# Whose engine subtracts the low halves: u, v and latent input projection weights, GpSimd to VectorE

## The chip, the cores and the metric

The kernel runs on one core of one Trainium2 chip. The core has a matrix engine (TensorE, "PE" in the profile, its weight loads "PEld"), VectorE ("DVE"), ScalarE ("ACT"), GpSimd ("POOL") and a queue that issues transfers (SyncE, "SP"). The metric is the time of one execution on the device in microseconds, the median of the runs.

## The reference

One layer of a hybrid diffusion backbone is applied to 256 context tokens and 1024 latent tokens with a model width of 1024. A token passes through a modulated norm, one input projection, windowed attention and a recurrent branch, an output projection with residual, a second norm, and a retrieval over 16384 experts. Each of 8 heads picks 16 experts e with weights g, and the mixer adds

```python
u = jnp.take(u_tab, eid, axis=0)
act = jax.nn.gelu(jnp.einsum('td,thkd->thk', xb, u))
vv = jnp.take(v_tab, eid, axis=0)
return jnp.einsum('thk,thkd->td', g * act, vv)
```

All of it is in float32.

## The kernel before

**Products in three passes.** TensorE carries a 12-bit mantissa exactly in one pass, so `split` (L132) writes an operand as a sum of two parts: ScalarE copies it into the high half (L134), and another engine subtracts the high half from the operand (L135). `mm3` (L138 to L140) then makes three products: high by high, high weights by low, low weights by high. The engine of the subtract is the fourth argument of `split`: VectorE if none is given. Before the change, GpSimd subtracts for five kinds of operand: the weights of the latent input projection (`wl`, 14 tiles), the weights of the retrieval's queries (`wl` too, 32 tiles), the experts' rows `ul` (128 tiles) and `vl` (128 tiles). VectorE does so for the other operands, among them `al`, the gated activations, and the context projection's weights (`wl`, 14 tiles). All weight tiles have 128 partitions by 1024 columns.

**Two ways to compute the experts.** For six of the eight latent tiles of 128 tokens (768 tokens) all 16384 experts are computed densely on TensorE, in 128 chunks of 128 experts: `experts_in` makes u products (16 groups of 3 matmuls of 384 columns for a chunk, 48 in all), gelu on ScalarE (L756), the weights g (L757, VectorE), a split of the result, and 36 matmuls of 512 columns against v (tiles `res`, which stay in PSUM, and `rot`, which are copied out by ScalarE at L737 and added to `acc` by VectorE at L738). The other four tiles (two of context, two of latent tokens) gather the 128 chosen rows of u and of v for each token: GpSimd issues an indirect DMA for each (L826, L837), and VectorE does a multiply with sum (L829) or a multiply-add (L843) on the row, 128x1024 elements each. Up to seven rows are in flight.

**Order.** The stages run in this order: modulations, the context's own layer up to its picks, the latent input projection with the recurrent branch, attention, output projection and norm, the retrieval's queries, the spreading of the weights (`spread`), with the u products of the first 34 chunks taken ahead (from about 980 to 1670 us), and `dense` (from about 1695 us): 17 pairs of chunks whose u products are already there, then 47 pairs that still make theirs. The program is written in one order, and a planner puts each engine's instructions in a fixed order from its own estimate of durations; each engine then works in that order and waits for the others by semaphores. The gathers are paced by hand: `tick` counts microseconds of other work and lets the generator `mix` issue the next row when enough have gone by; the row's VectorE work is queued behind a VectorE instruction of the dense part (`paced`).

Two loaded tiles of u and of v are there at a time, two of `uh` and `ul`, three of `vh` and `vl`, and one of `w` in the latent projection.

Of the kernel before, what the change touches and what calls it, by code (L numbers as in the profile page):

```python
# [18 lines left out]
PSUM = bass.MemoryType.PSUM  # L19
# [3 lines left out]
D = 1024  # L23
# [13 lines left out]
SCALE = HD ** -0.5  # L37
# Pairs (a, b) of ranks that can be among the 16 largest sums: (a + 1)(b + 1) <= 16.
SEGS = [(0, 1, 16), (1, 1, 8), (2, 1, 5), (3, 1, 4), (4, 1, 3), (5, 3, 2), (8, 8, 1)]
NC = sum(n * b for _, n, b in SEGS)  # L40
# Latent tiles whose experts are computed densely on the tensor engine; the others gather rows.
N_DENSE = 6
N_GATHER = N_LAT - N_DENSE
TD = N_DENSE * P
# Dense output tiles that stay in PSUM, chunks of experts whose products share an accumulation, chunks
# whose first products are taken ahead, gathered rows in flight (and more of them beside the dense part).
N_RES = 2
# [3 lines left out]
N_MORE = 3  # L51
# Pacing of the gathers: microseconds of other work per row and per part of that work.
F_STEP = 1.9
# [4 lines left out]
PE_US = 15.8  # L58
# The engine that divides a head's row by its sum.
NORM = "AAGV"  # L60
# [4 lines left out]
def body(ctx: ExitStack, tc: tile.TileContext, i, o):  # L65
# [44 lines left out]
    def tick(us, ins=None):  # L110
        """Gathers that may run beside us microseconds of the other work."""
        clock[0] += us
        if ins is not None:
            behind.append(ins.ins)
        ph = cur[0]
        step = D_STEP if ph == "dense" else STEP.get(ph, F_STEP)
        while queue and clock[0] >= step:
            try:
                next(queue[0])
                clock[0] -= step  # L120
            except StopIteration:
                queue.pop(0)
        if not queue:
            clock[0] = 0.0
# [7 lines left out]
    def split(hi, lo, src, eng=None):  # L132
        """src as the sum of two parts of 12 bits that one pass of a product carries exactly."""
        A.activation(hi, src, AF.Copy)  # L134
        return (eng or V).tensor_tensor(lo, src, hi, op=OP.subtract)  # L135
# [6 lines left out]
    def rstd_of(ss, p):  # L142
        """(ss / D + EPS) ** -0.5, with a Newton step."""
        m = p.tile([P, 1], F32, name="rs_m", bufs=3)
        V.tensor_scalar(m, ss, 1.0 / D, EPS, op0=OP.mult, op1=OP.add)
        r = p.tile([P, 1], F32, name="rs_r", bufs=3)
        G.tensor_tensor(r, m, nhalf, op=OP.pow)
        s = p.tile([P, 1], F32, name="rs_s", bufs=3)
        V.tensor_scalar(s, r, r, m, op0=OP.mult, op1=OP.mult)
        V.tensor_scalar(s, s, -0.5, 1.5, op0=OP.mult, op1=OP.add)  # L150
        V.tensor_tensor(r, r, s, op=OP.mult)
        return r

    # ---- modulations of both conditions: four blocks of 512 columns beside each other in the array,
    # block j in the rows 32 j (context) and 32 j + 1 (latent)
    def modulations(es):
        """A generator: the first part gives shift and scale of the first norm, the second the rest."""
        nonlocal ident
# [50 lines left out]
    def mod_row(t, cond, v):  # L209
        """Gate 1 (v = 0) or gate 2 (v = 1) for every token."""  # L210
        nc.sync.dma_start(t, modd[cond:cond + 1, v * D:(v + 1) * D].to_broadcast([P, D]))
        return t

    # ---- RG-LRU constants: -8 * softplus(-lambda) / 2, its negative, halved gate biases
    def lru_constants():
# [27 lines left out]
    def to_columns(ps, f, x, hh, hl, us, a, b, cond, nv=0):  # L243
        """A normed tile with the model dimension on the partitions, scaled, shifted and split."""
        for kk in range(2):
# [12 lines left out]
    def project(es, cond, qT, gy, kT, vv, xr, after=None):  # L258
        """The input projection; after(m) follows the columns m."""
        lat, pre, S, n, _, x_in, NB = dims(cond)  # L260
# [21 lines left out]
        hp = pool(es, pre + "hp")  # L282
        # columns of w_in: q (4 chunks), k, v, xr (4), yg (4)
        for m in (6, 10, 7, 11, 4, 5, 8, 12, 9, 13, 0, 1, 2, 3):
# [3 lines left out]
            wl = hp.tile([P, KD, P], F32R, name="wl", bufs=2)  # L288
            split(wh, wl, w, G if lat else V)
            for b in range(S // NB):  # L290
# [31 lines left out]
    def rotate(hp, ps, src):  # L322
        """Rotary embedding of two heads of all latent tokens, in place."""
        if not rope:
# [13 lines left out]
    def recur(cond, st, ps, gy, xr, blocks=range(4)):  # L338
        lat, _, S, _, _, _, NB = dims(cond)
        for c in blocks:  # L340
# [7 lines left out]
            for d in range(2):  # L348
# [12 lines left out]
                pl = lru[:, c, 2 + d:3 + d]  # L361
                # 1 - a^2 = tanh(-log a) (1 + a^2)
                A.activation(bv, av, AF.Tanh, scale=pl, bias=pl)
# [21 lines left out]
    def attend(cond, st, ps, tiles, qT, kT, vv, spare=None):  # L385
        lat, _, S, n, _, _, _ = dims(cond)
        base = S_CTX if lat else 0
        if lat:
            vc = load("vc", [P, 2, P], st)
            # keys split in two: the high part of a group's twice, the low part beside the group's half  # L390
            flat = [x.rearrange("p k t -> p (k t)") for x in spare]
# [10 lines left out]
        for t in tiles:  # L402
# [9 lines left out]
            for g in range(2):  # L412
# [5 lines left out]
                for c in range(4):  # L418
                    h = g * 4 + c
                    s = ps.tile([P, 2, 512] if lat else [P, W], F32, name="s", bufs=3 if lat else 2)  # L420
                    qh = qT[gs, c, ts]
                    # keys in columns: the cached context (latent tokens only), then the band
                    if not lat:
# [40 lines left out]
    def finish(es, cond, tiles, qT, gy, dest):  # L464
        """Output projection, residual and second norm: x1 and, for tiles of gathered experts, h2 to
        DRAM; the norm with the model dimension on the partitions to dest(t)."""
        lat, pre, S, n, t_0, x_in, _ = dims(cond)
# [58 lines left out]

    # ---- product-key retrieval
    picks = {}
# [3 lines left out]
    def choose(sq, ps, groups, vl, cb):  # L532
        """The 16 largest keys of every head and half for the tokens of each group (tiles, hh, hl),
        by tile, and the experts of the first half of the heads."""
        found = {}
# [41 lines left out]
    def combine(st, vals, idxs, t, part):  # L577
        """The 16 largest sums of every head of a half: experts and softmax weights."""
        ms = slice(part * 2 * HH, (part + 1) * 2 * HH)
# [16 lines left out]
        for h in range(HH):  # L596
# [3 lines left out]
            V.match_replace(out=left[:, h, :], in_to_replace=top[:, h, 8:16], in_values=left[:, h, :], imm_value=-BIG)  # L600
        # softmax over the chosen, in the places of the candidates
        nm = st.tile([P, HH, 16], F32, name="nm")
# [7 lines left out]
        V.tensor_tensor(cand, cand, z[:, :, None].to_broadcast([P, HH, NC]), op=OP.mult)  # L610
        # the chosen in the order of their places: the place (7 bits) leads 24 bits, of which the
        # first word holds the expert and 10 bits of the weight, the second the weight's other 20
        flat = lambda x: x.rearrange("p h c -> p (h c)")
# [23 lines left out]

    # weights of all experts for the dense tiles: [pair of second keys][first key][token][2]
    gd = dram.tile([64, P, max(TD, P), 2], F32, name="gd")
# [4 lines left out]
    def spread(gb, ps, t, x):  # L644
        """The weights of tile t over all experts, to DRAM as columns x of gd."""
        eid, gw = picks[t]
# [45 lines left out]
    def experts_in(raw, nraw, c, hh, hl, out):  # L692
        """gelu(h2 . u) of the experts with second key c and every dense token, to out(columns)."""
        u = raw.tile([P, KD, P], F32, name="u", bufs=nraw)
        nc.sync.dma_start(u, i["ut"][c])
        uh = eu.tile([P, KD, P], F32R, name="uh", bufs=2)
        ul = eu.tile([P, KD, P], F32R, name="ul", bufs=2)
        split(uh, ul, u, G)
        for b in range(nb):
# [6 lines left out]
    def dense(tiles, hh, hl):  # L706
        with ExitStack() as es:
# [33 lines left out]
            for c0 in range(0, P, GROUP):  # L741
                group = []
                for c in range(c0, c0 + GROUP):
# [3 lines left out]
                    vl = wk.tile([P, D], F32R, name="vl", bufs=GROUP + 1)  # L747
                    split(vh, vl, v, G)
                    if c % 2 == 0:
# [46 lines left out]
    def end_rows(new, cond):  # L796
        """The second gate and the gain of the last norm for every token."""
        gfin = new()
        nc.sync.dma_start(gfin, i["gfin"][None, :].to_broadcast([P, D]))
        return mod_row(new(), cond, 1), gfin  # L800

    def final(t, y, x1, ga2, gfin):
        """Gated residual and the last norm of a tile."""
        (G if N_CTX + N_RES <= t < N_CTX + N_DENSE and t % 2 == 0 else V).tensor_tensor(y, y, ga2, op=OP.mult)
# [10 lines left out]
    def mix(t):  # L815
        """The experts of a tile by gathered rows, one yield for each gather."""
        eid, gw = picks[t]
# [95 lines left out]
    with ExitStack() as fs:  # L913
# [3 lines left out]
        with ExitStack() as ks:  # L917
# [34 lines left out]
            def dest(t):  # L952
                hh, hl, u = (hha, hla, t) if t < N_DENSE else (hhb, hlb, t - N_DENSE)
                return hh, hl, slice(u * P, (u + 1) * P)
# [65 lines left out]
def layout(x):  # L1020
    """The inputs as the program reads them, and constants of the shapes."""
    f = np.float32
# [70 lines left out]
```

## Time and profile before

| | |
|---|---|
| runs | 3814.61, 3830.61, 3831.82 us; median 3830.61 us |
| span of the profiled execution | 3810.7 us; its time as a run is not listed apart; the fastest of the runs is 3.9 us above the span, the median 19.9 us |
| TensorE (PE) busy | 3360.2 us, 88% of the span |
| VectorE (DVE) busy | 3337.9 us, 88% |
| GpSimd (POOL) busy | 2305.5 us, 61% |
| ScalarE (ACT) busy | 1452.4 us, 38% |
| mean rate of the transfers | 239 GB/s |

An engine is busy while it has an instruction under way, and an instruction that is held up on its way counts as busy as well. Matmuls overlap each other, so that a busy TensorE need not be one at its peak.

### The profile page before, as it was taken

To read this page: it belongs to the slowest core of one execution; us is meant where nothing else is said; L and a number is where in the kernel's file an instruction comes from. 1 tells how busy PE (TensorE), PEld (TensorE's weight loads), DVE (VectorE), ACT (ScalarE), POOL (GpSimd) and SP (SyncE) were. 2 spreads that over 40 slices of the span, in tenths; PEclk is the share of its full clock that TensorE was granted. 3 is DMA by queue.
4 is the path that set the end of the run, shared out by engine and by line. 5 is a ranking of instruction groups with operands and counts; after the bars stand their busy time and mean duration, and the time that the engine had idled before them with its cause. 6 is when DMAs were issued, how large, how long until landed. Compare 5 with 4: busy or idle time off the path is not lost.

```text
span 3810.7 us, 48687 instructions
## 1 busy us (share of the span) xinstructions
PE 3360.2 (88%) x16982; PEld 2714.7 (71%) x16982; DVE 3337.9 (88%) x6484; ACT 1452.4 (38%) x2270; POOL 2305.5 (61%) x1388
## 2 busy tenths in 40 slices
PE   7888869988798888878889999999999989999997
PEld 4476544433598877766667878888888878888786
DVE  4549886667889999958999999999999999999998
ACT  5634535543211345534333333333333333333333
POOL 0032664456611222136767888878888888888884
PEclk9799888999899999999999999999999999999998
DMA  8342654468810266778888888888888888888884
GB/s 331 119 148 81 216 208 140 146 214 292 278 45 23 79 193 197 209 244 305 299 298 282 287 299 288 305 294 300 298 292 292 298 302 298 292 297 296 293 302 175
DMA packets 344823, 910.34 MB, mean 239 GB/s; under 512 B 28664, under 2 KB 147064, under 8 KB 341504
## 3 DMA queue, kind: packets, MB, share of 16 engines
q0 software_dynamic: 147456, 536.94, 40.3%
q1 hardware_dynamic: 197120, 370.29, 29.3%
q8 instruction: 133, 2.18, 0.2%
q14 instruction: 114, 0.93, 0.1%
HBM read 830.55 MB, written 76.57 MB: 238 GB/s over the span
## 4 chain that ended last, share of the span: by engine, by line
DVE 29%; PE 23%; issue 10%; POOL 4%; DMA 2%; ACT 2%; SPq 0%; POOLq 0%; DVEq 0%; ACTq 0%
DVE acc L843 8%; PE u L138 5%; PE u L139 5%; PE u L140 5%; DVE row L829 4%; DVE acc L738 4%; DVE oh L676 2%; PE rot L138 2%; DVE oh L674 1%; DVE al L135 1%; DVE oh L677 1%; PE rot L140 1%; PE rot L139 1%; DVE oh L675 1%; POOL row L826 1%
## 5 line engine op out<-in xcount | busy, mean ns | idle before, releaser
L826 POOL DMA_INDIRECT row<-in_peer_u,eid x512 | 731.5, 1429 | 286.8 <-issue 81.1
L837 POOL DMA_INDIRECT row<-in_peer_v,eid x512 | 716.5, 1399 | 287.8 <-DVE acc L843 85.5
L843 DVE SCALAR_TENSOR_TENSOR acc<-row,w,acc 128x1024 f32<-128x1024 f32 x508 | 836.2, 1646 | 29.6 <-DMA row<-in_peer_v,eid 25.6
L829 DVE SCALAR_TENSOR_TENSOR row<-row,h 128x1024 f32<-128x1024 f32 x512 | 722.9, 1423 | 64.3 <-DMA row<-in_peer_u,eid 63.9
L138 PE MATMUL u<-hh,uh 128*128 128x384 f32 x2048 | 700.2, 342 | 12.7 <-ACT uh L134 9.5
L140 PE MATMUL u<-hh,ul 128*128 128x384 f32 x2048 | 698.8, 341 | 2.3 <-POOL ul L135 2.3
L139 PE MATMUL u<-hl,uh 128*128 128x384 f32 x2048 | 698.7, 341 | 0.0
L135 POOL TENSOR_TENSOR ul<-u,uh 128x1024 fp32r<-128x1024 f32 x128 | 335.4, 2635 | 369.9 <-ACT uh L134 353.9
L737 ACT ACTIVATE q<-rot 128x512 f32<-128x512 f32 x504 | 298.7, 596 | 675.6 <-DVE acc L738 373.0
L138 PE MATMUL rot<-vh,ah 128*128 128x512 f32 x1024 | 430.8, 421 | 115.7 <-ACT q L737 107.4
L738 DVE TENSOR_TENSOR acc<-q,acc 128x512 f32<-128x512 f32 x504 | 472.7, 943 | 36.2 <-ACT q L737 35.6
L139 PE MATMUL rot<-vl,ah 128*128 128x512 f32 x1024 | 411.5, 402 | 0.0
L140 PE MATMUL rot<-vh,al 128*128 128x512 f32 x1024 | 411.2, 402 | 0.0
L138 PEld LDWEIGHTS u<-hh,uh 128*128 128x128 f32 x2048 | 389.5, 190 | 18.1 <-ACT uh L134 10.4
L140 PEld LDWEIGHTS u<-hh,ul 128*128 128x128 f32 x2048 | 388.8, 190 | 3.7 <-POOL ul L135 2.7
L139 PEld LDWEIGHTS u<-hl,uh 128*128 128x128 f32 x2048 | 388.7, 190 | 2.2
L138 PEld LDWEIGHTS rot<-vh,ah 128*128 128x128 f32 x1024 | 199.5, 195 | 225.6 <-ACT q L737 188.3
L135 POOL TENSOR_TENSOR vl<-v,vh 128x1024 fp32r<-128x1024 f32 x128 | 330.5, 2584 | 27.9 <-ACT vh L134 25.9
L140 PE MATMUL mm<-hh,wl 128*128 128x256 f32 (+2 forms) x848 | 290.3, 343 | 7.4 <-POOL wl L135 5.7
L138 PE MATMUL mm<-hh,wh 128*128 128x256 f32 (+2 forms) x848 | 287.8, 339 | 5.0 <-ACT wh L134 5.0
L139 PE MATMUL mm<-hl,wh 128*128 128x256 f32 (+2 forms) x848 | 287.4, 339 | 0.0
L135 POOL TENSOR_TENSOR wl<-w,wh 128x1024 fp32r<-128x1024 f32 x46 | 113.4, 2467 | 242.4 <-ACT wh L134 242.3
(259 smaller groups left out, 6092.6 us busy)
## 6 DMA issues: line engine op xcount, KB each, us to landing
u<-in_ut SPq DMA_DIRECT2D x128, 512.0 KB, 4.3
v<-in_peer_v SPq DMA_DIRECT2D x128, 512.0 KB, 4.4
gd<-stg SPq DMA_DIRECT2D x12, 4096.0 KB, 16.4
gt<-gd SPq DMA_DIRECT2D x64, 768.0 KB, 7.6
w<-in_w_mod SPq DMA_DIRECT2D x24, 1024.0 KB, 7.6
w<-in_w_query SPq DMA_DIRECT2D x32, 512.0 KB, 3.7
w<-in_w_in SPq DMA_DIRECT2D x28, 512.0 KB, 5.0
ad<-a SPq DMA_DIRECT2D x68, 192.0 KB, 3.7
```

What stands on the lines that cost most here:

```text
L135: return (eng or V).tensor_tensor(lo, src, hi, op=OP.subtract)
L138: T.matmul(out, lhs[0], rhs[0], start=first, stop=False)
L139: T.matmul(out, lhs[0], rhs[1], start=False, stop=False)
L140: T.matmul(out, lhs[1], rhs[0], start=False, stop=last)
L674: V.tensor_tensor(o1.rearrange(four, j=2), io, pairs(k1t, ts), op=OP.is_equal)
L676: V.tensor_tensor(oh.rearrange(four, j=2), o2.rearrange(four, j=2), pairs(gh, ts), op=OP.mult)
L737: A.activation(q, p, AF.Copy)
L738: tick(share / (2 * (N_DENSE - N_RES)), V.tensor_tensor(y, q, y, op=OP.add))
L826: G.indirect_dma_start(out=u, out_offset=None, in_=i["peer_u"], in_offset=bass.IndirectOffsetOnAxis(ap=eid[:, k:k + 1], axis=0))
L829: V.scalar_tensor_tensor(u, u, 1.0, h2, op0=OP.mult, op1=OP.mult, accum_out=act[:, j:j + 1])
L837: G.indirect_dma_start(out=v, out_offset=None, in_=i["peer_v"], in_offset=bass.IndirectOffsetOnAxis(ap=eid[:, k:k + 1], axis=0))
L843: V.scalar_tensor_tensor(acc, v, w[:, j:j + 1], acc, op0=OP.mult, op1=OP.add)
```

## The change

Three calls of `split` lose their fourth argument, so that the low halves of `wl` (in the latent input projection alone), `ul` and `vl` are subtracted on VectorE. The retrieval's queries (`choose`) still use GpSimd. Nothing else that runs is changed; comments fall away.

```diff
         for m in (6, 10, 7, 11, 4, 5, 8, 12, 9, 13, 0, 1, 2, 3):
...
-            split(wh, wl, w, G if lat else V)
+            split(wh, wl, w)
...
     def experts_in(raw, nraw, c, hh, hl, out):
...
-        split(uh, ul, u, G)
+        split(uh, ul, u)
...
                     vl = wk.tile([P, D], F32R, name="vl", bufs=GROUP + 1)
-                    split(vh, vl, v, G)
+                    split(vh, vl, v)
```

## Rows read from the trace of the kernel before

**Rows 1.** Busy time by stretch: PE, PEld, DVE, ACT, POOL, clock, DMA share, GB/s.
```profile
1140.00:1520.00 380.00, 337.68 (x2487) 309.54 (x2485) 375.51 (x1830) 147.89 (x200) 76.83 (x26) 0.97 0.41 122
1725.00:2047.00 322.00, 269.26 (x1091) 207.78 (x1090) 311.52 (x339) 125.59 (x190) 225.65 (x132) 0.97 0.84 294
2047.00:3760.00 1713.00, 1610.15 (x7833) 1411.59 (x7833) 1637.99 (x1644) 565.41 (x867) 1473.79 (x879) 0.98 0.85 295
3080.00:3120.00 40.00, 36.74 (x182) 32.19 (x180) 39.02 (x32) 12.41 (x20) 31.25 (x20) 1.00 0.90 322
```
**Rows 2.** Waits, 2047 to 3760 us: who <- for whom, total us, times, longest.
```profile
ACT q L737 <- DVE acc L738: 325.2, 197, 4.5
...
ACT uh L134 <- PE u L139: 139.0, 41, 3.6
PE rot L138 <- ACT q L737: 92.7, 73, 4.8
...
DVE row L829 <- DMA row<-in_peer_u,eid: 12.3, 7, 4.0
...
DVE al L135 <- ACT ah L134: 3.7, 4, 0.9
```
**Rows 3.** VectorE's groups, 2047 to 3760 us: count | busy us, mean ns | idle before.
```profile
L843 DVE SCALAR_TENSOR_TENSOR acc<-row,w,acc 128x1024 f32<-128x1024 f32 x350 | 608.2, 1738 | 3.7 <-DMA row<-in_peer_v,eid 1.0
L829 DVE SCALAR_TENSOR_TENSOR row<-row,h 128x1024 f32<-128x1024 f32 x345 | 505.3, 1477 | 12.3 <-DMA row<-in_peer_u,eid 12.3
L738 DVE TENSOR_TENSOR acc<-q,acc 128x512 f32<-128x512 f32 x375 | 369.4, 985 | 32.9 <-ACT q L737 32.8
L757 DVE TENSOR_TENSOR a<-a,gt 128x768 f32<-128x768 f32 x93 | 106.1, 1141 | 17.3 <-ACT a L756 17.2
L135 DVE TENSOR_TENSOR al<-a,ah 128x768 fp32r<-128x768 f32 x94 | 102.7, 1093 | 3.7 <-ACT ah L134 3.7
```
**Rows 4.** The same five by line, same stretch: ns shortest/median/longest, first and last start.
```profile
L843 DVE SCALAR_TENSOR_TENSOR acc<-row,w,acc x350: 1266/1277/5903, 2070.2 to 3752.6; 128x1024 f32<-128x1024 f32 x175
L829 DVE SCALAR_TENSOR_TENSOR row<-row,h x345: 1206/1212/6149, 2045.8 to 3712.1; 128x1024 f32<-128x1024 f32 x173
L738 DVE TENSOR_TENSOR acc<-q,acc x375: 672/679/5575, 2050.1 to 3759.8; 128x512 f32<-128x512 f32 x188
L757 DVE TENSOR_TENSOR a<-a,gt x93: 944/951/6166, 2054.5 to 3746.9; 128x768 f32<-128x768 f32 x93
L135 DVE TENSOR_TENSOR al<-a,ah x94: 942/950/3150, 2047.0 to 3749.0; 128x768 fp32r<-128x768 f32 x94
```
**Rows 5.** Timeline of VectorE and GpSimd around 3012 us: start, us, instruction.
```profile
3011.93 5.88 DVE L843 SCALAR_TENSOR_TENSOR acc<-row,w,acc 128x1024 f32<-128x1024 f32 x1
...
3011.96 4.76 POOL L135 TENSOR_TENSOR ul<-u,uh 128x1024 fp32r<-128x1024 f32 x2
```
**Rows 6.** GpSimd's subtracts, 2047 to 3760 us: count | busy us, mean ns | idle before.
```profile
L135 POOL TENSOR_TENSOR vl<-v,vh 128x1024 fp32r<-128x1024 f32 x94 | 239.9, 2553 | 1.6
L135 POOL TENSOR_TENSOR ul<-u,uh 128x1024 fp32r<-128x1024 f32 x92 | 230.1, 2522 | 0.9
```
**Rows 7.** VectorE's own subtract of that shape, from the context projection: ns shortest/median/longest.
```profile
L135 DVE TENSOR_TENSOR wl<-w,wh x14: 1218/1224/1226, 43.0 to 109.7; 128x1024 fp32r<-128x1024 f32 x14
```
**Rows 8.** Timeline of TensorE 2508 to 2515 us: start, us, matmul.
```profile
2508.47 0.63 PE L139 MATMUL rot<-vl,ah 128*128 128x512 f32 x1
2508.89 0.63 PE L140 MATMUL rot<-vh,al 128*128 128x512 f32 x1
...
2510.60 0.39 PE L140 MATMUL rot<-vh,al 128*128 128x512 f32 x1
2510.83 0.40 PE L138 MATMUL rot<-vh,ah 128*128 128x512 f32 x1
...
2512.21 0.34 PE L139 MATMUL u<-hl,uh 128*128 128x384 f32 x1
...
2514.12 0.34 PE L138 MATMUL u<-hh,uh 128*128 128x384 f32 x1
```
**Rows 9.** Two VectorE groups of `spread` with one shape, whole run: count | busy, mean.
```profile
L676 DVE TENSOR_TENSOR oh<-oh,tw 128x1024 f16<-128x1024 f16 x96 | 82.8, 862 | 7.2 <-PE g L680 7.2
...
L675 DVE TENSOR_TENSOR oh<-iota,tw 128x1024 f16<-128x1024 f16 x96 | 65.4, 681 | 0.0
```

## The prediction

> **What bounds the kernel now.** I read the busy time by stretch first. The steady part of the dense stage, 47 pairs of chunks from 2047 to 3760 us, is 1713 us long, 45% of the span. VectorE is busy for 1638 us of it, TensorE for 1610, GpSimd for 1474, and the transfers take 0.85 of their engines' time [rows 1]. Three engines look nearly full, so the busy shares alone do not say which one sets the pace. The waits do: ScalarE's copies out of PSUM (L737) wait 325 us for VectorE's additions (L738), and TensorE's `rot` products wait 93 us for these copies, while VectorE waits only 12 us for gathered rows [rows 2]. The chain goes from VectorE through ScalarE to TensorE, so VectorE sets the pace.
>
> Next I asked whether VectorE's 1638 us are work. Its five large groups have means far above their medians: 1738 ns against 1277 (L843), 1477 against 1212 (L829), 985 against 679 (L738), 1141 against 951 (L757), 1093 against 950 (`al`) [rows 3, 4]. The shortest of each lies within 10 ns of the median and the longest goes to 6 us, so most are undisturbed and a few are held up. The timeline shows by what: a multiply-add that usually takes 1.28 us took 5.88 us, and it began 0.03 us before two GpSimd subtracts that took 4.76 us together [rows 5]. 1.28 and 4.76 make 6.04: the one stood while the other two ran. The instructions that this change removes from GpSimd are thus the ones that stop VectorE.
>
> **What the held time amounts to.** Count times (mean less median) gives 350 x 0.461 = 161 us for L843, 345 x 0.265 = 91 for L829, 375 x 0.306 = 115 for L738, 93 x 0.190 = 18 for L757 and 94 x 0.143 = 13 for `al` [rows 3, 4], in all 399 us. The stretch has 94 + 92 = 186 GpSimd subtracts [rows 6], so each holds up VectorE by 399 / 186 = 2.14 us.
>
> Each such subtract lasts 2.55 or 2.52 us [rows 6], so most but not all of it is paid by VectorE. The Trainium skill (SBUF — State Buffer, "Who interferes with whom") says that a VectorE instruction with two SBUF inputs and a GpSimd instruction that reads SBUF take turns at a shared port, that whichever starts first keeps it for its whole length, and that the other stands still. Were all 186 paid in full, the held time would be 470 us in place of the 399 that the rows give; VectorE would be 71 us emptier still, and since TensorE is the bound by then (below), the forecast would not move.
>
> **What the change costs VectorE.** The subtract of this shape takes 1.224 us on VectorE, with 8 ns between the shortest and the longest of 14 [rows 7]. In the steady stretch 186 x 1.224 = 228 us come to VectorE's queue and 399 us of standing go: 1638 - 399 + 228 = 1467 us. With the 75 us for which VectorE is idle now (1713 - 1638, [rows 1]) it could finish in 1542 us.
>
> **What takes over.** TensorE. At full clock (2.4 GHz) eleven steps between matmuls of 384 columns take 1.91 us (2512.21 to 2514.12), 0.173 us each, and one of 512 columns follows the one before after 0.23 us (2510.60 to 2510.83) [rows 8]. A chunk has 48 and 36 of them, so 94 chunks take at least 94 x (48 x 0.173 + 36 x 0.23) = 780 + 778 = 1558 us. That is 91 us above VectorE's 1467. TensorE now loses 1713 - 1558 = 155 us: partly to waits on the copies, partly to the lower clock, at which the same matmul takes 0.42 us (2508.47 to 2508.89, [rows 8]); a granted clock of 0.98 [rows 1] means 0.02 x 1713 = some 30 us. The bounds of the loss that stays are 0 and 155. I take 45, the clock's part and a further 15: VectorE's load falls from 1638 / 1713 = 0.96 to 1467 / 1603 = 0.92, so the additions come sooner, but with a load that high they still come late at times. The stretch then takes 1603 us, **110 less** (0 to 155).
>
> **The other stretches.** In the first part of `dense` (1725 to 2047 us) VectorE is busy for 311.5 of 322 us [rows 1], and 34 chunks bring one subtract of v each. With the price above each frees 2.14 - 1.22 = 0.92 us, 31 us together, and VectorE with its idle time would need 291 us. TensorE's 1091 matmuls [rows 1] need 1091 x 0.23 = 251 us. The transfers run at a share of 0.84 here, and the densest 40 us that I looked at had 0.90 [rows 1]: at that share the stretch takes 322 x 0.84 / 0.90 = 300 us. I take that, **22 less** (5 to 31).
>
> From 1140 to 1520 us VectorE is busy for 375.5 of 380 us [rows 1], and most of the 34 early subtracts of u fall in or beside this stretch. Here the trace shows less held time: the f16 group L676 averages 862 ns where its sister L675 of the same shape has 681, 96 x 0.181 = 17 us [rows 9], and many of the other VectorE instructions there are not of this kind. If nothing is freed the change costs 34 x 1.22 = 41 us, if each frees 2.14 us it gives 31 us. I take **5 less**.
>
> The 14 subtracts of the latent projection cost 17 us on VectorE if nothing is freed and give 13 if each frees 2.14 us. They lie among VectorE's recurrence and context retrieval, and no row here decides which; I take 0. GpSimd's queue is relieved in all stretches (470 us in the steady one, [rows 6]), so rows are asked for earlier; I count that as nothing, since VectorE waits only 12 us for them [rows 2].
>
> **The sum.** 110 + 22 + 5 = 137 us from a span of 3810.7 gives 3674 us. The runs lie 4 to 21 us above that span, so I add 14: **3688 us**, against a median of 3830.6.
>
> **The rivals.**
>
> *VectorE stands at the head of its queue (slower).* GpSimd could wait for a high half without holding anything but gathers; on VectorE the subtract is one of a fixed order, and behind it are the row work and the additions that free TensorE's PSUM tiles. ScalarE itself waits for TensorE before 41 of the `uh` copies, 139 us or 3.4 us each [rows 2]. VectorE has 1713 - 1542 = 171 us to give away, 171 / 186 = 0.92 us for each subtract; above that the steady stretch gets longer. At 1.2 us each it takes 1542 + 223 = 1765 us (52 more), the first part 291 + 41 = 332 (10 more): 3893 us. Against it: VectorE's own subtract `al`, which hangs on a ScalarE copy in just this way, waited 3.7 us in 94 [rows 2]; ScalarE is busy for a third of the time [rows 1], so it is usually there first. 8 in 100. At about 0.8 us of waiting the first part's gain and the steady part's remnant come to within 0.5% of no change: 6 in 100.
>
> *The transfers hold it.* The stretch now runs at 295 GB/s, and 40 us at 322 GB/s [rows 1] do not show that this can be kept up. With a ceiling of 305 GB/s the steady stretch takes 1713 x 295 / 305 = 1657 us, the first part 322 x 294 / 305 = 310: 56 + 12 = 68 us less, some 3760 us. For it: the seven rows in flight are used as they come free. Against it: VectorE's 12 us of waiting for rows. 13 in 100.
>
> *Only part of it comes.* VectorE keeps pace with 0.5 us of new waiting per subtract: 1542 + 93 = 1635 us, 78 less, and 5 to 10 from the first part: about 3745 us, and up to 3800 where the early stage pays its 41 us besides. 10 in 100.
>
> *The change frees nothing.* If the long VectorE instructions had another cause, the 228 us and the first part's 41 would come on top of a full engine: about 4100 us. The timeline [rows 5] speaks plainly against it. 2 in 100.
>
> **How the numbers follow.** My forecast has 61 in 100, with a range of its own from 3640 (the stretch near its floor of 1558 us and the first part at 291) to 3735 (90 us of TensorE's loss stay). The range of 8 in 10 takes in the two smaller gains: 3640 to 3800. It leaves out the slower cases, most of "no change" and a few in 100 below. About 0.5%, 19 us, is what a measurement of this kernel can tell from no change, so faster means below 3811: 61 + 13 + 10 = 84 in 100; same 6; slower 10.
>
> **What would show it.** In the profile after: L843, L829 and L738 with means within some 2% of 1277, 1212 and 679 ns; `ul` and `vl` on VectorE at 1.22 us; GpSimd's busy time in the steady stretch down by some 470 us; pairs of chunks at 1603 / 47 = 34 us in place of 36.4; TensorE busy for 95% or more of the steady stretch, and ScalarE's wait for the additions well under 325 us. The forecast is wrong if VectorE shows long idle times ahead of `ul` or `vl` put down to ScalarE's `uh` or `vh` (first rival), or ahead of L829 and L843 put down to the DMA (second), or if TensorE waits for `ul` and `vl`.

## The result, and the profile after

The changed kernel takes **3740.4 us** (median of four runs, 3726.67 to 3749.55) against 3831.2 us before: a ratio of 0.9768, 95% interval 0.9739 to 0.9797. The forecast was 3688 us with a range of 3640 to 3800. Direction and range were right, and 91 us came in place of 143. The stages show that this is no small miss of one term, but two large ones of opposite sign.

The page of the changed kernel: busy time by engine, then the span in 40 slices, in tenths.
```profile
PE 3357.2 (90%) x16982; PEld 2758.1 (74%) x16982; DVE 3093.7 (83%) x6754; ACT 1454.8 (39%) x2266; POOL 1584.4 (42%) x1118
...
PE   7888879888798566899899999999999999999997
...
DVE  4549985767799989961599989998999999999997
...
POOL 0022453556521000000255656665666666666662
PEclk9799977999899755899999999999999999999998
```
GpSimd is down from 2306 to 1584 us, and VectorE, which got 270 instructions more, is down from 3338 to 3094. But slices 14 to 16 show a hole: TensorE at 5 and 6 tenths with its clock at 7 and 5, and then, in slice 19, VectorE at 1 tenth while TensorE is at 9.

To see what each stage gained I marked five events in each trace: ScalarE's first `uh` copy (the early u products begin), its 1st `vh` copy (the dense stage begins), its 37th (from there on every chunk makes its u products too), its 128th and last, and the end. Microseconds of the profiled executions:

| | first uh | early stage to first vh | to 37th vh | to 128th vh | tail | span |
|---|---|---|---|---|---|---|
| before | 981.9 | 713.0 | 376.7 | 1688.6 | 50.5 | 3810.7 |
| after | 961.0 | 855.1 | 335.8 | 1545.4 | 50.5 | 3747.8 |
| difference | -21 | **+142** | -41 | **-143** | 0 | -63 |

(The profiled execution of before was among its faster ones, that of after its slowest; hence 63 in place of 91 between them.)

Busy time by stretch after: in the spread, after it, in the first part of the dense stage, and in its steady part (columns as in [rows 1]).
```profile
1310.00:1640.00 330.00, 243.96 (x1995) 203.31 (x1994) 301.01 (x870) 141.03 (x162) 0.00 (x0) 0.72 0.59 168
1660.00:1800.00 140.00, 134.80 (x760) 134.36 (x761) 20.82 (x17) 32.53 (x50) 2.84 (x3) 0.96 0.39 126
1816.00:2152.00 336.00, 309.59 (x1290) 240.03 (x1291) 317.46 (x423) 145.37 (x219) 177.34 (x115) 0.98 0.91 327
2152.00:3697.00 1545.00, 1531.19 (x7709) 1385.00 (x7708) 1417.26 (x1799) 563.49 (x853) 959.68 (x684) 1.00 0.90 324
```
In the steady part TensorE is busy for 99% and its granted clock is 1.00, against 94% and 0.98 [rows 1]. The transfers reach 324 GB/s over 1545 us. The first two lines are the hole: 330 us in which TensorE is busy for 244 at a clock of 0.72, then 140 us in which it works nearly alone.

VectorE's groups in the steady part after (answers to [rows 3]): count | busy, mean ns | idle before.
```profile
L843 DVE SCALAR_TENSOR_TENSOR acc<-row,w,acc 128x1024 f32<-128x1024 f32 x349 | 446.0, 1278 | 0.1
L829 DVE SCALAR_TENSOR_TENSOR row<-row,h 128x1024 f32<-128x1024 f32 x336 | 404.3, 1217 | 8.5 <-DMA row<-in_peer_u,eid 8.5
L738 DVE TENSOR_TENSOR acc<-q,acc 128x512 f32<-128x512 f32 x368 | 251.9, 685 | 53.8 <-ACT q L737 53.8
L135 DVE TENSOR_TENSOR ul<-u,uh 128x1024 fp32r<-128x1024 f32 x93 | 113.4, 1220 | 59.1 <-ACT uh L134 59.1
L135 DVE TENSOR_TENSOR vl<-v,vh 128x1024 fp32r<-128x1024 f32 x92 | 111.6, 1217 | 0.0
```
The means have fallen onto the medians of before (1277, 1212 and 679 ns, [rows 4]), and the subtract costs what [rows 7] said. The wait at the head of VectorE's queue exists, 59 us for 93 `ul`, or 0.64 us each, but it is paid out of VectorE's spare time (it is busy for 1417 of 1545 us).

Waits of the same stretch after (answers to [rows 2]): total us, times, longest.
```profile
ACT q L737 <- PE rot L140: 258.8, 215, 4.5
...
ACT q L737 <- DVE acc L738: 81.3, 69, 3.7
```
ScalarE's copies waited 325 us for VectorE before and wait 81 us now; mostly they wait for TensorE. The bound has moved as forecast.

In the spread, TensorE's u products and its f16 products after (1310 to 1640 us): count | busy, mean ns | idle before.
```profile
L680 PE MATMUL g<-oh,oh 128*128 128x128 f16 x752 | 142.5, 267 | 35.4 <-DVE oh L676 35.1
...
L140 PE MATMUL u<-hh,ul 128*128 128x384 f32 x160 | 58.5, 368 | 0.7 <-DVE ul L135 0.6
```
and VectorE's second f16 group beside them:
```profile
L676 DVE TENSOR_TENSOR oh<-oh,tw 128x1024 f16<-128x1024 f16 x94 | 64.6, 688 | 27.1 <-PE g L680 26.8
```
The same stretch of the kernel before, by engine and for the same two groups of TensorE:
```profile
1310.00:1640.00 330.00, 293.95 (x2492) 256.31 (x2493) 324.11 (x935) 166.02 (x204) 69.93 (x22) 0.98 0.64 189
```
```profile
L140 PE MATMUL u<-hh,ul 128*128 128x384 f32 x354 | 126.2, 356 | 0.0
...
L680 PE MATMUL g<-oh,oh 128*128 128x128 f16 x706 | 99.7, 221 | 22.0 <-DVE oh L676 21.4
```
16 matmuls of L140 belong to a chunk, so 10 chunks' u products were made in these 330 us. Before it was 354 matmuls, or 22 chunks, with TensorE busy for 294 us at a clock of 0.98. And VectorE's timeline after the spread:
```profile
1702.74 1.22 DVE L135 TENSOR_TENSOR ul<-u,uh 128x1024 fp32r<-128x1024 f32 x1 [7.10 <-ACT uh L134]
1711.06 1.22 DVE L135 TENSOR_TENSOR ul<-u,uh 128x1024 fp32r<-128x1024 f32 x1 [7.10 <-ACT uh L134]
```
The missing chunks are made here, one every 8.3 us, TensorE's own time for 48 matmuls at 0.173 us. VectorE has nothing else to do and stands for 7.1 us between two subtracts. What ran side by side before now runs one after the other. By the trace's count of these matmuls, 18.9 of the 34 chunks are still to be made when the last f16 product ends, against 2.3 before: 16.6 x 8.3 = 138 us, nearly all of the 142.

### The profile page after: what moved, and what is told of

Same layout as the page of the kernel before. It is cut to its first block, busy times and chain, and to the rows that moved or that the text cites. A ratio compares the mean times of both kernels' runs of the same rounds, so it can differ in the third digit from the quotient of the medians.

```text
span 3747.8 us, 48586 instructions
## 1 busy us (share of the span) xinstructions
PE 3357.2 (90%) x16982; PEld 2758.1 (74%) x16982; DVE 3093.7 (83%) x6754; ACT 1454.8 (39%) x2266; POOL 1584.4 (42%) x1118
## 4 chain that ended last, share of the span: by engine, by line
PE 39%; DVE 7%; issue 2%; DMA 2%; POOL 1%; ACT 0%; DVEq 0%; POOLq 0%; ACTq 0%
PE u L140 7%; PE u L139 7%; PE u L138 7%; PE rot L138 4%; PE rot L140 4%; PE rot L139 4%; PE res L140 2%; PE res L139 2%; PE res L138 2%; DVE row L829 2%; DVE acc L738 2%; DVE acc L843 1%; DMA a<-ad 1%; POOL row L826 1%; DMA row<-in_peer_u,eid 1%
## 5 line engine op out<-in xcount | busy, mean ns | idle before, releaser
L837 POOL DMA_INDIRECT row<-in_peer_v,eid x512 | 700.7, 1369 | 993.9 <-DMA ad<-a 458.2
L140 PE MATMUL u<-hh,ul 128*128 128x384 f32 x2048 | 699.0, 342 | 49.8 <-DVE ul L135 49.7
L843 DVE SCALAR_TENSOR_TENSOR acc<-row,w,acc 128x1024 f32<-128x1024 f32 x508 | 651.8, 1283 | 26.3 <-DMA row<-in_peer_v,eid 25.0
L829 DVE SCALAR_TENSOR_TENSOR row<-row,h 128x1024 f32<-128x1024 f32 x512 | 624.0, 1231 | 47.0 <-DMA row<-in_peer_u,eid 46.7
L140 PEld LDWEIGHTS u<-hh,ul 128*128 128x128 f32 x2048 | 390.4, 191 | 55.6 <-DVE ul L135 54.1
L138 PE MATMUL rot<-vh,ah 128*128 128x512 f32 x1024 | 406.2, 399 | 18.9 <-ACT q L737 13.2
L139 PE MATMUL rot<-vl,ah 128*128 128x512 f32 x1024 | 399.3, 391 | 0.0
L140 PE MATMUL rot<-vh,al 128*128 128x512 f32 x1024 | 398.7, 391 | 0.0
L738 DVE TENSOR_TENSOR acc<-q,acc 128x512 f32<-128x512 f32 x504 | 341.9, 684 | 55.1 <-ACT q L737 55.0
L135 DVE TENSOR_TENSOR ul<-u,uh 128x1024 fp32r<-128x1024 f32 x128 | 156.1, 1219 | 184.3 <-ACT uh L134 184.2
L140 PE MATMUL mm<-hh,wl 128*128 128x256 f32 (+2 forms) x848 | 289.6, 342 | 5.7 <-POOL wl L135 2.9
L134 ACT ACTIVATE uh<-u 128x1024 fp32r<-128x1024 f32 x128 | 135.7, 1060 | 389.4 <-PE u L139 355.9
L140 PEld LDWEIGHTS rot<-vh,al 128*128 128x128 f32 x1024 | 192.9, 188 | 41.4
```

The costliest lines, as they stand in the source:

```text
L138: T.matmul(out, lhs[0], rhs[0], start=first, stop=False)
L139: T.matmul(out, lhs[0], rhs[1], start=False, stop=False)
L140: T.matmul(out, lhs[1], rhs[0], start=False, stop=last)
L738: tick(share / (2 * (N_DENSE - N_RES)), V.tensor_tensor(y, q, y, op=OP.add))
L829: V.scalar_tensor_tensor(u, u, 1.0, h2, op0=OP.mult, op1=OP.mult, accum_out=act[:, j:j + 1])
L837: G.indirect_dma_start(out=v, out_offset=None, in_=i["peer_v"], in_offset=bass.IndirectOffsetOnAxis(ap=eid[:, k:k + 1], axis=0))
```

## The experiments

The kernel before was timed anew beside each group of runs, at 3834 to 3835 us; ratios are to that.

**Early u back to GpSimd.** Only the 34 chunks that are taken ahead go back.

```diff
-    def experts_in(raw, nraw, c, hh, hl, out):
+    def experts_in(raw, nraw, c, hh, hl, out, eng=None):
...
-        split(uh, ul, u)
+        split(uh, ul, u, eng)
...
-            experts_in(vl, 1, c, hha, hla, keep_act)
+            experts_in(vl, 1, c, hha, hla, keep_act, G)
```

> The changed kernel with the low halves of u of the 34 chunks taken ahead (the early stage) subtracted on GpSimd again; the wl of the latent projection, the u of the other 94 chunks and all v stay on VectorE. Theory A (queue order: on VectorE these 34 subtracts stand behind the work of spread in a fixed queue, so that TensorE has no u products to do beside spread and does them alone afterwards): the early stage, from the first uh copy to the first vh copy, goes back from 855 us to some 713 us, the dense stage keeps its 1932 us, the whole takes about 3610 us. Theory B (the stage is longer by the time of the added instructions, 34 x 1.22 us, and by other changes of the plan that have nothing to do with where u is subtracted): no more than some 40 us come back, 3700 us.

Measured: **3608.4 us**, ratio to before 0.9407 (0.9378 to 0.9436). The early stage takes 724.9 us, the steady part 1544.8. This is the fastest kernel of the study, 132 us below the changed one. Its spread, by stretch:
```profile
1310.00:1640.00 330.00, 294.78 (x2561) 256.55 (x2560) 323.58 (x893) 167.18 (x201) 65.86 (x21) 0.99 0.69 202
```
TensorE has its 295 us and its clock of 0.99 again.

**Only the early u on VectorE**, the rest as before.

```diff
-        split(uh, ul, u, G)
+        split(uh, ul, u, eng)
...
-                        experts_in(wk, 2, c, hh, hl, lambda bs, p: ...)
+                        experts_in(wk, 2, c, hh, hl, lambda bs, p: ..., G)
```

> The kernel before with the 34 early subtracts of u alone moved to VectorE; all else on GpSimd. Theory A: the early stage gets some 140 us longer, nothing else changes, about 3965 us (a slowdown of 3 to 4%). Theory B: at most 41 us longer, 3830 to 3870 us.

Measured: 3959.8 us, ratio 1.0346 (1.0306 to 1.0385), 126 us slower. The early stage takes 845.4 us (132 more), and each other stage lies within 5 us of before. Its u products in the spread:
```profile
L140 PE MATMUL u<-hh,ul 128*128 128x384 f32 x165 | 60.3, 368 | 0.7 <-DVE ul L135 0.6
```
165 in place of 354, as after the change. So 34 instructions of 1.2 us (41 us of VectorE) cost about 130 us, and from both sides it is these 34.

**The early chunks written between the tiles of the spread**, all subtracts on VectorE.

```diff
         for x, t in enumerate(dt):
             if x + 1 < N_DENSE:
                 combine(cb, *found[t + 1], t + 1, 1)
+            for c in range(EARLY * x // N_DENSE, EARLY * (x + 1) // N_DENSE):
+                experts_in(vl, 1, c, hha, hla, keep_act(c))
             spread(sp, pp, t, x)
...
-        for c in range(EARLY):
...
```

> The changed kernel, all three kinds of subtract on VectorE, with the 34 early chunks written into the program between the six tiles of spread (0, 5, 11, 17, 22, 28 chunks ahead of a tile's spread) in place of after them all. Theory A: what cost the time is the place in VectorE's queue, so that the early stage shrinks although the subtracts stay on VectorE: 720 to 750 us, the whole 3620 to 3650 us. Theory B (VectorE has no room for them in a stage in which it is full): the spread is stretched by as much as TensorE gains, no more than 40 us come back, 3700 us or more.

Measured: 3674.2 us, ratio 0.9578 (0.9542 to 0.9613); 66 us below the changed kernel, half of what e1_early_g gives. The early stage takes 789.1 us. By stretch, and two VectorE groups of that stretch:
```profile
1310.00:1725.00 415.00, 366.40 (x2848) 329.52 (x2849) 327.03 (x919) 180.93 (x220) 0.00 (x0) 0.89 0.59 173
```
```profile
L676 DVE TENSOR_TENSOR oh<-oh,tw 128x1024 f16<-128x1024 f16 x94 | 64.7, 688 | 58.3 <-PE g L680 58.2
...
L135 DVE TENSOR_TENSOR ul<-u,uh 128x1024 fp32r<-128x1024 f32 x28 | 34.3, 1224 | 24.2 <-ACT uh L134 24.0
```
The place in the program, with nothing moved off VectorE, is worth half: theory A holds for that half. The other half is lost in a new way. VectorE, in its fixed order, now stands in the middle of the spread for TensorE (58 us) and for ScalarE's high halves (24 us); the last f16 product of the spread ends at 1726 us in place of 1644. GpSimd is busy for 66 us of the spread's 330 in e1_early_g, with these subtracts alone, so that its waiting for `uh` stopped nothing else.

**The latent projection's wl on GpSimd too**, on top of e1_early_g.

```diff
-            split(wh, wl, w)
+            split(wh, wl, w, G if lat else V)
```

> As e1_early_g, with the 14 wl of the latent projection on GpSimd as well, so that only the dense stage differs from the kernel before. If the 21 us by which the changed kernel reaches its first uh copy earlier come from wl: 20 us slower than e1_early_g, about 3630 us. If wl makes no difference: the same as e1_early_g within 8 us.

Measured: 3647.2 us, ratio 0.9506 (0.9474 to 0.9537), 39 us above e1_early_g with intervals that do not touch. The first `uh` copy comes at 995.5 us against 953.2; the stages behind it differ by some 5 us at most. VectorE from 314 to 560 us, first with wl on GpSimd, then on VectorE:
```profile
L829 DVE SCALAR_TENSOR_TENSOR row<-row,h 128x1024 f32<-128x1024 f32 x32 | 44.0, 1392 | 16.3 <-DMA row<-in_peer_u,eid 16.3
L843 DVE SCALAR_TENSOR_TENSOR acc<-row,w,acc 128x1024 f32<-128x1024 f32 x23 | 31.4, 1367 | 9.4 <-DMA row<-in_peer_v,eid 9.2
...
L372 DVE TENSOR_TENSOR gi<-bv,gi 128x1024 f32<-128x1024 f32 x8 | 13.0, 1621 | 1.1 <-ACT bv L370 1.1
```
```profile
L829 DVE SCALAR_TENSOR_TENSOR row<-row,h 128x1024 f32<-128x1024 f32 x32 | 40.9, 1300 | 3.6 <-DMA row<-in_peer_u,eid 3.6
L843 DVE SCALAR_TENSOR_TENSOR acc<-row,w,acc 128x1024 f32<-128x1024 f32 x17 | 21.8, 1283 | 2.2 <-DMA row<-in_peer_v,eid 2.0
...
L372 DVE TENSOR_TENSOR gi<-bv,gi 128x1024 f32<-128x1024 f32 x8 | 9.8, 1226 | 0.0
```
With wl on GpSimd the recurrence's `gi` is 0.4 us longer each, as an instruction that is made to stand would be, and the waits for rows are 26 us in place of 6. How the 39 us divide between the two was not separated, and the 39 are themselves uncertain by some 10: the first `uh` copy comes at 982 to 996 us in the three profiles with this wl on GpSimd (before, e2_only_early_v, e3_wl_g), and at 936 to 961 us in the seven with it on VectorE and the queries' on GpSimd.

**A GpSimd subtract ahead of VectorE's own**, in the dense stage of e1_early_g; VectorE then writes the true value.

```diff
+        if eng is None:
+            G.tensor_tensor(ul, u, u, op=OP.subtract)
         split(uh, ul, u, eng)
...
+                    G.tensor_tensor(vl, v, v, op=OP.subtract)
                     split(vh, vl, v)
```

> e1_early_g with one GpSimd subtract added ahead of each VectorE subtract of u and v in the dense stage: it writes the operand minus itself (zeros) into the low half's tile, and the VectorE subtract then writes the true value over it. VectorE's own instructions are those of e1_early_g. Theory A (a GpSimd instruction that reads two tiles makes VectorE stand still for nearly its length): the means of L843, L829 and L738 go back to about 1740, 1480 and 985 ns from 1280, 1220 and 680, each added instruction takes some 2.1 us from VectorE, a pair of chunks takes 37.1 + 4 x 1.22 = 42 us in place of 34, the whole about 4050 us. Theory B (the held time came from something else that fell away with the change, such as later gathers or waits inside the instruction): the means stay, and as GpSimd has room for 10 us more in a pair of 34 us, the time stays near 3610 us.

**Two GpSimd fills in its place**, which read nothing.

```diff
+        if eng is None:
+            G.memset(ul.bitcast(F32), 0.0)
+            G.memset(ul.bitcast(F32), 0.0)
         split(uh, ul, u, eng)
...
+                    G.memset(vl.bitcast(F32), 0.0)
+                    G.memset(vl.bitcast(F32), 0.0)
                     split(vh, vl, v)
```

> e1_early_g with two GpSimd fills with zero (no input tile) added ahead of each VectorE subtract of u and v in the dense stage, into the low half's tile, which the VectorE subtract then overwrites. If only a GpSimd instruction that reads the on-chip memory holds up VectorE: the means of L843, L829 and L738 stay within 3% of 1280, 1220 and 680 ns, and the time stays at about 3610 us (3600 to 3640). If any GpSimd instruction holds it up: the means rise by the fills' length, to about 1500, 1350 and 830 ns at 1 us for a fill, and the time to 3700 us or more.

Measured: 3943.4 us with the subtract (ratio 1.0275, 1.0228 to 1.0323) and 3868.3 us with the fills (1.0085, 1.006 to 1.0111). VectorE's three large groups in the steady part, with the subtract and then with the fills (L846, L832, L740 and L848, L834, L741 are L843, L829, L738):
```profile
L846 DVE SCALAR_TENSOR_TENSOR acc<-row,w,acc 128x1024 f32<-128x1024 f32 x350 | 541.9, 1548 | 0.1
L832 DVE SCALAR_TENSOR_TENSOR row<-row,h 128x1024 f32<-128x1024 f32 x336 | 459.0, 1379 | 6.5 <-DMA row<-in_peer_u,eid 6.4
L740 DVE TENSOR_TENSOR acc<-q,acc 128x512 f32<-128x512 f32 x368 | 289.4, 787 | 1.4 <-ACT q L739 1.3
```
```profile
L848 DVE SCALAR_TENSOR_TENSOR acc<-row,w,acc 128x1024 f32<-128x1024 f32 x349 | 446.3, 1279 | 2.4 <-DMA row<-in_peer_v,eid 2.3
L834 DVE SCALAR_TENSOR_TENSOR row<-row,h 128x1024 f32<-128x1024 f32 x336 | 405.1, 1219 | 101.4 <-DMA row<-in_peer_u,eid 101.3
L741 DVE TENSOR_TENSOR acc<-q,acc 128x512 f32<-128x512 f32 x367 | 250.8, 686 | 11.1 <-ACT q L740 10.3
```
On the means the answer is clear: reading stretches VectorE's instructions, filling does not (1279, 1219, 686 ns; 1284, 1223, 691 in e1_early_g). Theory A's sizes were too high: 1740, 1480 and 985 ns were expected, and 1548, 1379 and 787 came. On the time the expectation for the fills failed by 230 us: the kernel got slower with VectorE undisturbed. Waits with the fills, 2007 to 3801 us:
```profile
DVE ul L135 <- POOL ul L700: 90.9, 23, 6.6
POOL ul L699 <- PE u L140: 89.8, 35, 7.0
```
The fill waits until TensorE has read the tile, the gathers stand behind the fill in GpSimd's queue (VectorE waits 101 us for rows of u), VectorE's low half waits for the fill, and TensorE 63 us for the low half. So the times of this pair cannot be set down to the standing still, and I built it again without that tie.

**The same two beside the work**: the instructions write a tile of their own that nobody reads. TensorE's and VectorE's planned orders are those of e1_early_g, instruction by instruction.

```diff
+    def beside(x):
+        d = spare_tile[0].tile([P, 960], F32, name="beside")
+        G.tensor_tensor(d, x[:, :960], x[:, :960], op=OP.subtract)
...
         split(uh, ul, u, eng)
+        if eng is None:
+            beside(u.rearrange("p k t -> p (k t)"))
...
                     split(vh, vl, v)
+                    beside(v)
```

> e1_early_g with one more GpSimd instruction for each tile of u and v in the dense stage: it reads the loaded tile twice (960 of 1024 columns) and writes zeros into a tile of its own that nothing reads, so that no other engine waits for it; the planned order of TensorE and VectorE is that of e1_early_g. Theory A (a GpSimd instruction that reads holds VectorE up): the means of L843, L829 and L738 rise by 150 to 450 ns, VectorE's busy time in a pair of chunks goes from 31 to 38 or 39 us, above TensorE's 33, and the whole takes 3800 to 3920 us. Theory B (GpSimd's instructions cost time only through what waits for them, the gathers and the low halves): the means stay, and the time stays within 30 us of 3608, since GpSimd is busy for 62% of the steady stretch and nothing waits for the added instructions.

```diff
-        G.tensor_tensor(d, x[:, :960], x[:, :960], op=OP.subtract)
+        G.tensor_copy(d[:, 0:1], x[:, 0:1])
+        G.memset(d, 0.0)
+        G.memset(d, 0.0)
```

> As e8_read_beside, but the GpSimd instructions beside are a copy of one column of the loaded tile (which ties them to its arrival) and two fills with zero of 960 columns, which read nothing: about 2 us of GpSimd for each tile, nearly as much as in e8_read_beside. If only reading holds VectorE up: means as in e1_early_g (1284, 1223, 691 ns, within 3%), time within 30 us of 3608. If GpSimd's time as such costs (gathers asked for later behind it): as slow as e8_read_beside within 1%.

Measured: 3881.1 us with the reads (ratio 1.0124, 1.0075 to 1.0173), 3780.5 us with the fills (0.985, 0.9801 to 0.9899), against 3608.4 without either. The steady part takes 1763.7 and 1703.2 us against 1544.8. VectorE's groups there and the added instructions, with the reads:
```profile
L853 DVE SCALAR_TENSOR_TENSOR acc<-row,w,acc 128x1024 f32<-128x1024 f32 x350 | 521.1, 1489 | 0.1
L839 DVE SCALAR_TENSOR_TENSOR row<-row,h 128x1024 f32<-128x1024 f32 x336 | 465.5, 1397 | 23.9 <-DMA row<-in_peer_u,eid 23.1
L747 DVE TENSOR_TENSOR acc<-q,acc 128x512 f32<-128x512 f32 x368 | 297.7, 809 | 1.6 <-ACT q L746 1.6
...
L696 POOL TENSOR_TENSOR beside<-v 128x960 f32<-128x960 f32 x91 | 207.2, 2276 | 104.0 <-DMA v<-in_peer_v 102.2
```
and with the fills:
```profile
L855 DVE SCALAR_TENSOR_TENSOR acc<-row,w,acc 128x1024 f32<-128x1024 f32 x349 | 447.4, 1282 | 103.0 <-DMA row<-in_peer_v,eid 102.5
L841 DVE SCALAR_TENSOR_TENSOR row<-row,h 128x1024 f32<-128x1024 f32 x336 | 407.3, 1220 | 147.0 <-DMA row<-in_peer_u,eid 139.5 <-issue 6.7 <-DVE acc L749 0.5
L749 DVE TENSOR_TENSOR acc<-q,acc 128x512 f32<-128x512 f32 x368 | 252.3, 686 | 4.8 <-ACT q L748 4.3 <-ACT vh L134 0.6
...
L698 POOL MEMSET beside<- 128x960 f32 x184 | 167.4, 910 | 5.7
L697 POOL MEMSET beside<- 128x960 f32 x184 | 166.1, 902 | 10.5
L696 POOL COPY beside<-v 128x1 f32<-128x1 f32 x92 | 75.9, 825 | 48.2 <-DMA v<-in_peer_v 45.4
```
Theory A is shown by the means: 1489, 1397 and 809 ns against 1282, 1220 and 686 (L738 gains 118 ns over e1_early_g, less than the 150 expected), with the same planned order and about as much GpSimd time (408 and 470 us added in the steady part). But the second expectation failed on the time: the fills cost 172 us, neither at most 30 nor as much as the reads (273). VectorE's instructions are undisturbed, and it waits 242 us for gathered rows (102.5 + 139.5). The 470 us put GpSimd back to 1434 busy us of 1703, or 0.84, near the 0.86 it had before [rows 1]. With a GpSimd queue that full the rows come too late; in e1_early_g these waits are 8 us. Part of it may be another thing: the small copy that ties the fills to a tile waits 45 us for the load of v at the head of that queue (the added subtract waits 102 us in e8_read_beside), most of the copies' 137 busy us is waiting for VectorE (last section), and the gathers stand behind. No run separates this from the fills' own time.

**The queries' wl on VectorE as well**, the last of the four kinds of operand that GpSimd subtracted before: the remaining `split(wh, wl, w, G)` in `choose` loses its fourth argument, on top of e1_early_g.

> e1_early_g with the 32 weight tiles of the retrieval's queries subtracted on VectorE too, so that GpSimd keeps the 34 early u alone. VectorE is freed of up to 2.1 us and pays 1.22 us each: 32 x 0.9 = 29 us at best, 3580 us, if they stay near the front of its queue; if they stand behind other VectorE work there, as the early u did, TensorE waits for its query products and the time rises, 3620 to 3680 us. I expect the first for the 16 of the context (which run beside the latent projection) and nothing from the other 16: 3595 us.

Measured: 3626.3 us, ratio 0.9457 (0.9408 to 0.9506), the interval overlapping that of e1_early_g: the hoped-for 13 us did not come, and whether it loses is not settled. In its profile the first `uh` copy comes at 968.7 us, later than the 936 to 961 of the seven kernels above, and the stages behind it are as long as in e1_early_g within 3 us.

## Why the prediction was right in sign and range, and where it failed

**The time: in the range, in part by luck.** Against the sum of 137 us, the steady part gave 33 more, the first part of the dense stage 19 more and the time up to the first `uh` copy 21 more, while the early stage was off by 147 the other way: 137 + 73 - 147 = 63, the difference of the two profiles. Without the 73 us that I had not counted, the miss of the early stage would have put the time at 3688 + 147 = 3835 us, no change at all. One rival, that only part of it comes, stands at 3745 us, near the measured 3740; its reason, 0.5 us of waiting for each subtract and 78 us less in the steady part, is not what happened, since the steady part gave 143.

**VectorE stands still while GpSimd subtracts: right.** In the steady stretch of the kernel before, VectorE's instructions lasted 411 us longer in sum than the median of their kind, and 410 of these lie in instructions that overlap a GpSimd subtract in time. (The shortest L843 lies 11 ns below its median, not within 10.) The means fell to the medians of before, and e8_read_beside brought the stretching back with reads that nobody waits for. Fills do not do it. The Trainium skill (SBUF — State Buffer, "Who interferes with whom") says just this: a VectorE instruction with two inputs in SBUF contends with a GpSimd instruction that reads SBUF, not with one that only writes it. The runs agree: 1489 ns for L843 beside reads, 1282 beside fills. Which of the two stands is less simple than the prediction's "whichever starts first", if the recorded starts are taken for it: the multiply-add of [rows 5] began 0.03 us before the subtracts and was the one that stood. Of the L843 and L829 of that stretch that were under way when a subtract began, 60 of the 61 that had begun up to 0.4 us before stood for over 2 us; none of the 65 that had begun 0.6 to 1.0 us before did.

**1.22 us for the subtract on VectorE: right** (1220 and 1217 ns).

**TensorE becomes the bound, 1603 us for the steady stretch: right in mechanism, mis-sized.** 110 us were forecast and 143 came. Per pair of chunks, 1545.4 / 45.5 = 34.0 us against a forecast of 34.1; before it was 1688.6 / 45.5 = 37.1, where I had 36.4 by counting 47 pairs into a window that holds about 46. The mis-sized term is TensorE's loss above its 33.1 us of matmuls for a pair (1558 / 47): 4.0 us before and 0.8 after, where the sum had 3.3 and 1.0. The loss that I let TensorE keep for its clock (30 us) went too: the granted clock is 1.00.

**The first part of the dense stage, 22 less: came to 41.** The transfers reached the share that I took as the ceiling (0.91 at 327 GB/s), but the stage up to the 37th `vh` copy was 377 us long, more than the 322 us I had put into the sum: 377 x 294 / 327 = 339 us, near the 336 measured. Whether the transfers set the pace there was not tested.

**GpSimd's relief counts as nothing: wrong.** I had read that VectorE waits only 12 us for rows [rows 2] and concluded that the gathers had room. They had it for a VectorE that was slow. e9_write_beside gives GpSimd about its old load back with VectorE free: VectorE waits 242 us for rows, and the kernel is 172 us slower. As far as this run shows (the copies' own waits are in it), the change took away two bounds that lay nearly on top of each other, and it needed both to go. Bringing the reads back costs 101 us more than the fills (3881.1 - 3780.5).

**From 1140 to 1520 us, 5 less: this is the step that failed.** It cost 142 us in the profile, and 132 between the medians of the changed kernel and e1_early_g. I priced the 34 early subtracts by their durations, with bounds from -31 to +41 us, and the result lies far outside. What counts there is the place in the queue. On GpSimd, busy for 70 of 330 us there, a subtract ran as soon as its high half was there, and TensorE made u products beside the spread. On VectorE they stand in an order that puts the spread's work first; TensorE has 10 chunks in place of 22 to do, its clock falls to 0.72, its f16 products get slower (267 ns against 221), and VectorE's L676 waits 27 us for them. The u products then follow alone. I had named this case among the signs ("if TensorE waits for `ul` and `vl`") without a price; the rival that I did price had VectorE wait for its operands, and that, 0.64 us for each `ul`, did no harm.

**The latent projection, 0: wrong**, by 39 us between e3_wl_g and e1_early_g (21 between the profiles before and after), again outside bounds made of instruction times (17 us of cost to 13 of gain). What the sum lacked is open: longer VectorE instructions and later rows were both seen.

**The rivals.** The ceiling of 305 GB/s is refuted by 324 GB/s over 1545 us; that the change frees nothing, by the means.

## What to carry to other kernels

An elementwise instruction that moves to another engine has three prices: its time there, what it held up where it was, and its place in the new engine's fixed queue. The third has to be read stage by stage: in the profiles the same edit gained 184 us in the dense stage, where VectorE's queue was short of nothing but time, and lost 142 us where VectorE was full of work that the plan puts first, and the best kernel moves the subtracts in the one stage and leaves them in the other. And a queue with no waits behind it may be covered by the bound that is about to be removed: before counting its relief as nothing, ask whether it could serve the faster engine.

## What the runs showed of the hardware that was not expected

- GpSimd's copy of one column (128x1) took 0.66 and 0.83 us on average (`beside` from u and from v in e9_write_beside), nearly as much as a fill of 960 columns (0.91 us). Most of that is waiting for VectorE. The 32 copies that began while no VectorE instruction of over 0.5 us was under way took 0.18 to 0.20 us; of the 135 that took 0.3 us or more, 134 ended 0.03 to 0.06 us after such an instruction did. One of them, which began in an L855 and ended 0.05 us after the L749 behind it:
```profile
2908.84 1.27 DVE L855 SCALAR_TENSOR_TENSOR acc<-row,w,acc 128x1024 f32<-128x1024 f32 x1
...
2909.15 1.61 POOL L696 COPY beside<-v 128x1 f32<-128x1 f32 x1
...
2910.03 0.68 DVE L749 TENSOR_TENSOR acc<-q,acc 128x512 f32<-128x512 f32 x1
```
- Gathers and loads together kept 324 GB/s for 1545 us at a share of 0.90, where the kernel before had 295 [rows 1].
- TensorE's granted clock was 0.72 between 1310 and 1640 us of the changed kernel, where it made short f16 products with gaps, and 0.98 or 0.99 in the same stretch of the two kernels that fed it u products.
